# Four closing transposes of a triangular inverse as pieces of their own in an interleaved two-layer backbone kernel

## The chip, the core and the metric

The kernel runs on one core of one Trainium2 chip. The metric is the device time of one execution in microseconds (us). TensorE (PE) does the matmuls, VectorE (DVE), ScalarE (ACT) and GpSimd (POOL) the rest; SyncE (SP) and POOL issue most transfers. Each engine runs its own instructions in the order in which they stand in its stream.

## The reference

The reference is a flow-matching backbone of two layers over 512 latent tokens of width 1024, with a prefix of 256 context tokens. The even layer has two grouped-query attentions, the odd layer a 2-D neighbourhood attention beside a bidirectional recurrence (RWKV-7). Each layer ends in a SwiGLU. The part that matters here is the recurrence, run forward and backward over first the context and then the latent tokens, for 8 heads of 64:

```python
def wkv7_scan(state0, p, d, reverse, emit):
    ...
    def step(S, inp):
        w_t, k_t, v_t, kk_t, a_t = inp[:5]
        sa = jnp.einsum('bhvk,bhk->bhv', S, kk_t)
        S = (S * w_t[:, :, None, :] - sa[..., None] * (kk_t * a_t)[:, :, None, :]
             + v_t[..., None] * k_t[:, :, None, :])
        return S, (jnp.einsum('bhvk,bhk->bhv', S, inp[5]) if emit else None)

    s_fwd, yc_fwd = wkv7_scan(zero, cx, 0, False, need_ctx)
    s_bwd, yc_bwd = wkv7_scan(zero, cx, 1, True, need_ctx)
    _, y_fwd = wkv7_scan(s_fwd, lat, 0, False, True)
    _, y_bwd = wkv7_scan(s_bwd, lat, 1, True, True)
```

## The kernel before

**Dense work.** A projection takes its weights in tiles of 128 output columns. SP loads a tile (`wraw`), ACT casts it to a high part (`whi`, L143), DVE subtracts for the low part (`wlo`, L145), two buffers each. PE then forms three products: high by high (L422), activation low by weight high (L423), high by weight low (L424). L119 and L124 split an activation in the same way.

**The recurrence in chunks of 32 tokens.** For the context (256 tokens) and for each of two groups of latent tokens, `prepare` builds decay products (L1231 to L1250 on ACT and DVE), the scaled keys `kb` (L1242), the Gram blocks `G` (matmul L1258, mask L1262) and their transposes (L1260). Then `rwkv_inverse` inverts 32 unit triangular blocks of 32x32 per head half and direction: two POOL memsets (L1291, L1292), four DVE transposes from `G` (L1295), 31 rank-1 steps of a product and a subtraction (L1299, L1302), and four transposes of the result back into `G` (L1307). It is a generator that pauses after every second rank-1 step, 15 times. The caller then spills `G` to HBM (L1515, SP), from where `rwkv_load` (L1323) fetches each chunk's operands for the scan.

**The scan.** One step handles one chunk for both directions: W from VU and Sd (matmuls L1351, L1357, copies L1361, L1365), VU from W (L1370, L1373), the new state S (L1380, L1381), its scaled copies Sd (L1384) and, for latent tokens, the outputs (L1389, L1391).

**What sets the order.** The work is written as Python generators, and one runs beside another by counts: a main loop calls `step(n)` after each of its pieces, and the aside generator is advanced by the whole part of what it is owed. In layer 0's FFN the aside is the context chain (its projections, its inverse, its scan), advanced by 1.6 pieces for each FFN piece (L968), with a modulation row beside it for every second piece (L956). `finish` flushes what is left behind layer 1's first norm. In layer 1, latent group 0 advances the dense projections by 0.1 for each inverse piece (L1636). Group 1 is interleaved with the first half of the latent scan: after each scan piece it is owed 1.75 pieces, and each of them advances the dense projections by 1.4 (L1645 to L1652). A list scheduler then reorders the instructions of a block by its own costs. `keep_in_program_order` adds an edge without a semaphore: its instruction may not stand ahead of the instruction written before it on the same engine. The modulation rows (L278) have it already.

**After group 1** the neighbourhood attention starts beside the second half of the scan: scores (L1087), their bias and row maximum (L1092 on DVE), exponentials (L1093), transposes (L1099), copies of these (L1101 on DVE) and the products with the values (L678).

Of the kernel before, what the change touches and what calls it, by code (L numbers as in the profile page):

```python
# [69 lines left out]
class Net:  # L70
# [1203 lines left out]
    def rwkv_inverse(self, kbp, tp, Gs):  # L1274


        nc, V = self.nc, self.nc.vector
        L = self.t(kbp, [P, 1024], "kb").rearrange("p (a b) -> p a b", a=32)
        Xf = self.t(kbp, [P, 1024], "kb")
        X = Xf.rearrange("p (a b) -> p a b", a=32)  # L1280
        M = self.t(tp, [P, 256], "pi", bufs=1)

        def blocks(t, d, u):
            q = 32 * (2 * d + u)
            return t[q : q + 32, ::-1, ::-1] if d else t[q : q + 32]

        def inG(d, u):
            W = Gs[d].shape[3]
            return Gs[d][HD * u + 32 : HD * u + HD].rearrange("p c a t -> p t c a")[:, W - 32 : W]

        nc.gpsimd.memset(Xf, 0.0)  # L1291
        nc.gpsimd.memset(Xf[:, 0:1024:33], 1.0)  # L1292
        for d in range(2):
            for u in range(2):
                V.transpose(blocks(L, d, u), inG(d, u))  # L1295
        for j in range(31):
            n, m = 31 - j, j + 1
            t = M[:, 0 : n * m].rearrange("p (a b) -> p a b", a=n)
            V.tensor_tensor(  # L1299
                t, L[:, j + 1 : 32, j : j + 1].broadcast_to([P, n, m]), X[:, j : j + 1, 0:m].broadcast_to([P, n, m]), op=ALU.mult  # L1300
            )
            V.tensor_tensor(X[:, j + 1 : 32, 0:m], X[:, j + 1 : 32, 0:m], t, op=ALU.subtract)  # L1302
            if j % 2:
                yield
        for d in range(2):
            for u in range(2):
                V.transpose(inG(d, u), blocks(X, d, u))  # L1307

    def rwkv_state(self, sp):

# [517 lines left out]
```

## Time and profile before

| what | value |
|---|---|
| median of three runs | 2051.96 us (2051.79 to 2053.8) |
| profiled execution | 2053.72 us, of which span 2051.9 |
| PE busy | 1956.0 us (95%) |
| DVE busy | 1261.4 us (61%) |
| ACT, POOL busy | 893.7 us, 163.0 us |
| closing transposes (L1307) | 12, of 1877 to 2083 ns each |
| where they stand | 987 to 999 us (context), 1354.8 to 1362.8 (group 0), 1484.0 to 1491.7 (group 1) |

Times in rows of the timeline count from the start of the span, the second number is the duration in us. In brackets stand the idle time of that engine just before, and what ended it. A row with `x4` is a run of four instructions. The windows view gives busy times per engine for a stretch, then PE's granted clock as a share of full speed, then the busy share of the DMA engines and GB/s.

### The profile page before, as it was taken

To read this page: it belongs to the slowest core of one execution; us is meant where nothing else is said; L and a number is where in the kernel's file an instruction comes from. 1 tells how busy PE (TensorE), PEld (TensorE's weight loads), DVE (VectorE), ACT (ScalarE), POOL (GpSimd) and SP (SyncE) were. 2 spreads that over 40 slices of the span, in tenths; PEclk is the share of its full clock that TensorE was granted. 3 is DMA by queue.
4 is the path that set the end of the run, shared out by engine and by line. 5 is a ranking of instruction groups with operands and counts; after the bars stand their busy time and mean duration, and the time that the engine had idled before them with its cause. 6 is when DMAs were issued, how large, how long until landed. Compare 5 with 4: busy or idle time off the path is not lost.

```text
span 2051.9 us, 37913 instructions
## 1 busy us (share of the span) xinstructions
PE 1956.0 (95%) x15360; PEld 1606.6 (78%) x15360; DVE 1261.4 (61%) x2504; ACT 893.7 (44%) x1681; POOL 163.0 (8%) x326
## 2 busy tenths in 40 slices
PE   7999999999988999999999999899899989999997
PEld 6776778999987888777777777677667778888887
DVE  5656667666657554659746767787757773333335
ACT  4335556766733433553222346545345453222221
POOL 0111100000010001000112000102322000000000
PEclk9999999999999999999999999999799999999999
DMA  7453422434484345545533323455665133332321
GB/s 277 148 182 124 145 91 74 145 115 128 133 268 141 109 128 164 157 147 154 179 125 117 111 73 98 130 173 174 171 198 146 52 98 113 93 101 85 106 90 50
DMA packets 109918, 272.64 MB, mean 133 GB/s; under 512 B 14736, under 2 KB 48176, under 8 KB 106800
## 3 DMA queue, kind: packets, MB, share of 16 engines
q1 hardware_dynamic: 97520, 224.74, 35.5%
q0 software_dynamic: 12224, 45.49, 6.8%
q8 instruction: 121, 1.98, 0.4%
q14 instruction: 53, 0.43, 0.1%
HBM read 238.20 MB, written 31.98 MB: 132 GB/s over the span
## 4 chain that ended last, share of the span: by engine, by line
PE 78%; DVE 10%; issue 6%; DMA 3%; ACT 2%; POOL 0%; DVEq 0%; ACTq 0%; SPq 0%; POOLq 0%
PE ps_b L422 17%; PE ps_b L423 17%; PE ps_b L424 17%; PE ps_v L678 4%; PE ps_a L628 2%; PE ps_e L650 2%; PE ps_w L1351 2%; PE ps_w L1357 2%; DVE wlo L145 1%; PE ps_s L1380 1%; DMA xx<-in_wmod 1%; PE ps_w L1370 1%; PE ps_e L1258 1%; PE ps_w L1389 1%; DVE kb L1295 1%
## 5 line engine op out<-in xcount | busy, mean ns | idle before, releaser
L143 ACT CAST whi<-wraw 128x1024 fp32r<-128x1024 f32 (+2 forms) x291 | 292.6, 1008 | 664.1 <-PE ps_b L423 526.3
L145 DVE TENSOR_TENSOR wlo<-wraw,whi 128x1024 fp32r<-128x1024 f32 (+2 forms) x291 | 340.8, 1172 | 235.5 <-ACT whi L143 229.3
L422 PE MATMUL ps_b<-hxh,whi 128*128 128x512 f32 (+1 forms) x1040 | 402.4, 390 | 15.8 <-ACT cj L1018 6.7
L423 PE MATMUL ps_b<-hxl,whi 128*128 128x512 f32 (+1 forms) x1040 | 398.4, 385 | 2.1 <-DVE hxl L415 1.9
L424 PE MATMUL ps_b<-hxh,wlo 128*128 128x512 f32 (+1 forms) x1040 | 396.6, 383 | 2.2 <-DVE wlo L145 2.2
L422 PEld LDWEIGHTS ps_b<-hxh,whi 128*128 128x128 f32 x1040 | 199.1, 193 | 59.0 <-ACT cj L1018 7.2
L423 PEld LDWEIGHTS ps_b<-hxl,whi 128*128 128x128 f32 x1040 | 199.2, 192 | 40.7 <-DVE hxl L415 3.8
L424 PEld LDWEIGHTS ps_b<-hxh,wlo 128*128 128x128 f32 x1040 | 199.5, 193 | 39.7 <-DVE wlo L145 3.3
L422 PE MATMUL ps_b<-act,whi 128*128 128x512 f32 (+1 forms) x570 | 198.9, 349 | 6.5 <-ACT whi L143 3.3
L424 PE MATMUL ps_b<-act,wlo 128*128 128x512 f32 (+1 forms) x570 | 197.4, 346 | 2.1 <-DVE wlo L145 2.1
L423 PE MATMUL ps_b<-act,whi 128*128 128x512 f32 (+1 forms) x570 | 196.4, 345 | 0.4 <-DVE act L124 0.4
L422 PE MATMUL ps_b<-hch,whi 128*128 128x256 f32 x552 | 159.9, 290 | 4.2 <-ACT cj L982 2.1
L424 PE MATMUL ps_b<-hch,wlo 128*128 128x256 f32 x552 | 156.4, 284 | 0.8 <-DVE wlo L145 0.7
L423 PE MATMUL ps_b<-hcl,whi 128*128 128x256 f32 x552 | 156.0, 283 | 0.0
L422 PEld LDWEIGHTS ps_b<-act,whi 128*128 128x128 f32 x570 | 109.2, 192 | 21.7 <-issue 4.3
L424 PEld LDWEIGHTS ps_b<-act,wlo 128*128 128x128 f32 x570 | 109.1, 191 | 16.1 <-DVE wlo L145 3.3
L423 PEld LDWEIGHTS ps_b<-act,whi 128*128 128x128 f32 x570 | 109.1, 191 | 13.3 <-DVE act L124 0.8
L754 DVE TENSOR_TENSOR ff_a<-ff_a,ps_b 128x512 f32<-128x512 f32 x44 | 30.2, 687 | 134.3 <-PE ps_b L424 133.6
L422 PEld LDWEIGHTS ps_b<-hch,whi 128*128 128x128 f32 x552 | 104.9, 190 | 8.7 <-ACT cj L982 2.6
L424 PEld LDWEIGHTS ps_b<-hch,wlo 128*128 128x128 f32 x552 | 104.7, 190 | 1.9 <-DVE wlo L145 1.5
L455 DVE SCALAR_TENSOR_TENSOR xx<-ps_b,mod,xx 128x512 f32<-128x512 f32 (+1 forms) x64 | 43.7, 684 | 101.0 <-PE ps_b L424 100.6
L423 PEld LDWEIGHTS ps_b<-hcl,whi 128*128 128x128 f32 x552 | 105.1, 191 | 0.9 <-issue 0.2
(375 smaller groups left out, 3332.2 us busy)
## 6 DMA issues: line engine op xcount, KB each, us to landing
wraw<-in_ffi SPq DMA_DIRECT2D x132, 512.0 KB, 3.6
xx<-in_wmod POOLq DMA_DIRECT2D x48, 512.0 KB, 4.9
wraw<-in_w1in SPq DMA_DIRECT2D x43, 512.0 KB, 3.7
wraw<-in_ffo SPq DMA_DIRECT2D x48, 448.0 KB, 3.3
wmod<-in_wmodT POOLq DMA_DIRECT2D x32, 512.0 KB, 3.9
wraw<-in_ffo SPq DMA_DIRECT2D x24, 512.0 KB, 3.6
op<-op SPq DMA_DIRECT2D x32, 384.0 KB, 3.8
qx<-in_wmod SPq DMA_DIRECT2D x8, 1024.0 KB, 10.6
```

The costliest lines, as they stand in the source:

```text
L143: self.nc.scalar.copy(hi[:, 0:n], raw)
L145: e.tensor_tensor(lo[:, 0:n], raw, hi[:, 0:n].bitcast(F32), op=ALU.subtract)
L422: mm(out, lhsT=wh, rhs=hh, start=first, stop=False)
L423: mm(out, lhsT=wh, rhs=hl, start=False, stop=False)
L424: mm(out, lhsT=wl, rhs=hh, start=False, stop=last)
L455: self.nc.vector.scalar_tensor_tensor(X[:, m, c], ps[:, 0:n][:, c], gate[:, m, i : i + 1], X[:, m, c], op0=ALU.mult, op1=ALU.add)
L628: nc.tensor.matmul(o, lhsT=q, rhs=k[:, b : b + o.shape[1]], start=i == 0, stop=i == len(passes) - 1)
L650: nc.tensor.transpose(pt[:, P * (j - c) : P * (j - c) + P], p[:, P * j : P * j + P], self.ident)
L678: self.nc.tensor.matmul(ps[HD * u : HD * u + HD, col : col + P], lhsT=vs[u][j], rhs=pts[u][:, j, :], start=j == 0, stop=j == nk - 1, tile_ ...
L754: V.tensor_tensor(a, a, pg[1][:, 0:w], op=ALU.mult)
L1351: mm(wy[HD * u + HD - W_ + r : HD * u + HD, p, :], lhsT=G[top[u], p, r:W_], rhs=VU[top[u], p, u, :], start=p == 0, stop=False, skip_group_ ...
L1357: mm(o, lhsT=AR[:, p, :], rhs=Sd[:, p, u, :], start=False, stop=not lat, skip_group_check=True)
```

## The change

Each of the four closing transposes is tied behind the DVE instruction written just before it, and the generator pauses after each. The inverse so has 19 pauses instead of 15, in all three of its uses.

```diff
@@ -1304,7 +1304,8 @@
                 yield
         for d in range(2):
             for u in range(2):
-                V.transpose(inG(d, u), blocks(X, d, u))
+                self.tc.keep_in_program_order(V.transpose(inG(d, u), blocks(X, d, u)))
+                yield
 
     def rwkv_state(self, sp):
```

Lines from 1308 on are one higher in the changed kernel. The order of the instructions changes at three places and around them.

On DVE in the context's inverse, inside layer 0's FFN (`xx` is the residual stream, `wmod` a modulation row), the rows before:

```order
L1302 TENSOR_TENSOR kb_10271<-kb_10271,pi_10272 128x31
L1307 STREAM_TRANSPOSE G_1908_9355<-kb_10271 32x32x32
L455 SCALAR_TENSOR_TENSOR xx_7182<-ps_b_10565,mod_8_79,xx_7182 128x512
L145 TENSOR_TENSOR wlo_10638<-wraw_10635,whi_10637 128x896
L1307 STREAM_TRANSPOSE G_1908_9355<-kb_10271 32x32x32
L1307 STREAM_TRANSPOSE G_1909_9356<-kb_10271 32x32x32
L455 SCALAR_TENSOR_TENSOR xx_7182<-ps_b_10601,mod_8_79,xx_7182 128x512
L145 TENSOR_TENSOR wlo_10671<-wraw_10668,whi_10670 128x896
L1307 STREAM_TRANSPOSE G_1909_9356<-kb_10271 32x32x32
```

and of the change, from the second of its transposes on:

```order
L455 SCALAR_TENSOR_TENSOR xx_7182<-ps_b_10713,mod_8_79,xx_7182 128x512
L1307 STREAM_TRANSPOSE G_1908_9355<-kb_10271 32x32x32
L279 ISA wmod_10593,mod_9_80<-wmod_10593,silu_r_8030,c_tab_65 128x1024
L279 ISA mod_9_80 128x1
L1307 STREAM_TRANSPOSE G_1909_9356<-kb_10271 32x32x32
L145 TENSOR_TENSOR wlo_10775<-wraw_10772,whi_10774 128x1024
```

The first transpose keeps its place; the other three have moved behind the next weight tiles, and other work stands between each two of them. The context chain is four pieces longer with it: on PE, the L1351 and L1357 of its last step stood ahead of the last tiles of layer 0's FFN, and the last step but one and this one now stand behind them, among the matmuls of layer 1's first norm.

On ACT in latent group 0, two sets of decay operations and the evacuation of a dense tile (`cj` from PE's bank `ps_b`), before:

```order
L1240 ACTIVATE P_1522_7226<-sg_13859 128x8x32
L1231 ACTIVATE th_13911<-ps_e_13907,b0h_7220 128x256
L1231 ACTIVATE th_13911<-ps_e_13908,b0h_7220 128x256
L1233 ACTIVATE sg_13914<-th_13911,half_7218 128x256
L1235 ACTIVATE KA_13916<-th_13911,omka_7223,kah_7222 128x8x32
L1236 ACTIVATE KA_13916<-th_13911,half_7218 128x8x32
L1240 ACTIVATE P_1522_7226<-sg_13914 128x8x32
L1018 ACTIVATE cj_13937<-ps_b_13770 128x8x64
L143 CAST whi_14126<-wraw_14124 128x1024
```

and of the change:

```order
L1240 ACTIVATE P_1522_7226<-sg_13865 128x8x32
L143 CAST whi_14126<-wraw_14124 128x1024
L1018 ACTIVATE cj_13914<-ps_b_13770 128x8x64
L1231 ACTIVATE th_13934<-ps_e_13930,b0h_7220 128x256
L119 CAST cj_13913<-cj_13914 128x512
```

The cast and the evacuation have moved from behind the second set to ahead of it. On DVE, one `wlo` and one L124 now stand among the last rank-1 steps of that inverse, and its four transposes stand together as before.

On DVE at the end of latent group 1, where the attention's scores begin, before:

```order
L1092 ISA hxl_2795_15655,sm_m_15654<-ps_a_15651,cb_15588,big_15579 128x512
L1092 ISA sm_m_15654 128x1
L1302 TENSOR_TENSOR kb_14897<-kb_14897,pi_14898 128x31
L1092 ISA hxl_2800_15689,sm_m_15688<-ps_a_15685,cb_15588,big_15579 128x512
L1092 ISA sm_m_15688 128x1
L1307 STREAM_TRANSPOSE G_2577_13847<-kb_14897 32x32x32 x2
L1307 STREAM_TRANSPOSE G_2578_13848<-kb_14897 32x32x32 x2
L1101 COPY hxh_2801_15692<-ps_e_15693 128x512
```

and of the change:

```order
L1302 TENSOR_TENSOR kb_14910<-kb_14910,pi_14911 128x3x29
L1101 COPY hxh_2801_15692<-ps_e_15693 128x512
L1299 TENSOR_TENSOR pi_14911<-kb_14909,kb_14910 128x60
L1092 ISA hxl_2815_15783,sm_m_15782<-ps_a_15779,cb_15588,big_15579 128x512
L1092 ISA sm_m_15782 128x1
L1302 TENSOR_TENSOR kb_14910<-kb_14910,pi_14911 128x2x30
L1299 TENSOR_TENSOR pi_14911<-kb_14909,kb_14910 128x31
L1302 TENSOR_TENSOR kb_14910<-kb_14910,pi_14911 128x31
L1307 STREAM_TRANSPOSE G_2577_13853<-kb_14910 32x32x32 x2
L1307 STREAM_TRANSPOSE G_2578_13854<-kb_14910 32x32x32 x2
L1101 COPY hxh_2811_15772<-ps_e_15773 128x512
```

Before, two score operations stood ahead of the transposes and the first L1101 behind them. Now five score operations and the first L1101 stand among the rank-1 steps ahead of them, and the second L1101 behind.

## The prediction

> **What bounds the kernel now.** I read the page's engine totals first, then the windows around the three inverses, then the timeline inside those windows.
>
> ```profile
> PE 1956.0 (95%) x15360; PEld 1606.6 (78%) x15360; DVE 1261.4 (61%) x2504; ACT 893.7 (44%) x1681; POOL 163.0 (8%) x326
> L1307 DVE STREAM_TRANSPOSE G<-kb x12: 1877/1986/2083, 987.1 to 1489.8; 32x1024 f32<-32x1024 f32 x12
> ```
>
> TensorE is busy 95% of the span. A change that adds no matmul can gain only where PE stands idle, some 96 us in all, and can lose wherever it makes PE stand. The twelve closing transposes cost DVE 12 x 1.99 = 24 us; the change removes none of that. It moves them, and what stands around them.
>
> ```profile
> 1140.00:1160.00 20.00, 20.00 (x229) 15.69 (x228) 12.51 (x22) 5.95 (x11) 1.83 (x3) 1.00 0.25 80
> 1168.00:1192.00 24.00, 19.37 (x164) 16.51 (x158) 21.48 (x61) 11.37 (x24) 1.52 (x2) 0.93 0.36 132
> 1380.00:1400.00 20.00, 20.00 (x356) 15.25 (x357) 14.33 (x31) 10.09 (x25) 8.18 (x12) 1.00 0.63 179
> 1422.00:1441.00 19.00, 16.80 (x119) 13.00 (x116) 17.45 (x32) 3.96 (x7) 2.98 (x6) 0.82 0.68 200
> 1501.00:1620.00 119.00, 118.21 (x1707) 86.39 (x1704) 80.50 (x177) 61.80 (x145) 28.64 (x48) 1.00 0.43 121
> ```
>
> After each stretch stand its length, then busy us of PE, weight loads, DVE, ACT and POOL, then the granted clock. In the FFN of layer 0 (1140), between the two latent groups (1380) and in the attention (1501) PE is full at clock 1.00. What is gained ahead of such a stretch carries to the end. In layer 1's first norm (1168) DVE is the busy one: 21.48 of 24 us, with PE 4.63 us idle. Those idle places are what the change can touch.
>
> **Part A: the context inverse, the FFN and the norm.** The four pauses added here lengthen the aside generator by four pieces, and half-rate modulation rows run with it. The FFN advances the aside at its own rate, so its last pieces no longer fit. One whole step of the context scan and the first half of the next now stand behind the FFN, in the norm.
>
> ```profile
> 1154.69 0.64 PE L1351 MATMUL ps_w<-VU,op 32*32 32x64 f32 x16
> ...
> 1156.40 0.64 PE L1357 MATMUL ps_w<-Sd,op 128*32 128x64 f32 x16
> 1167.66 1.08 PE L1370 MATMUL ps_w<-W,op 32*32 32x64 f32 x32
> 1152.26 0.69 PE L1380 MATMUL ps_s<-VU,op 128*64 128x64 f32 x16
> 1192.09 0.50 PE L422 MATMUL ps_b<-hxh,whi 128*128 128x512 f32 x1 [1.88 <-ACT wa L1147]
> 1190.78 1.22 DVE L145 TENSOR_TENSOR wlo<-wraw,whi 128x1024 fp32r<-128x1024 f32 x1 [1.67 <-ACT whi L143]
> 1171.11 0.43 DVE L1373 COPY VU<-ps_w 32x256 f32<-32x256 f32 x1
> ```
>
> The first half of a step (four sets, from 1154.69 to 1157.04) takes 2.3 us of PE; L1370 takes 1.1, the two sets of L1380 2 x 0.69. So 4.8 us for a step and 2.3 for the half: 7.1 us leave a stretch where PE is full. The norm has 4.63 us of PE idle, so at least 2.5 of the 7.1 come back. DVE has as many S and Sd operations between its first and last hxl as before, since the new step takes the slot of the old one. But the second step's end now falls at the start of the dense phase: two W copies (2 x 0.43) ahead of the wlo of 1190.78, mostly in its 1.67 us idle, and two VU copies behind it. They end near 1190.78 + 1.22 + 0.86 = 1192.9. PE's L1380 waits for them ahead of the first dense matmul, which stood at 1192.09. With its own 0.7 that puts the dense start at 1193.6, 1.5 us late. I take A = 7.1 - 2.5 - 1.5 = **+3.1 us**. Bounds: +4.6 if the late copies hide, and -4 if none of the 7.1 hides (0) and a load is waited for (3.8, below). The spread transposes are worth at most the stall behind them:
>
> ```profile
> 996.07 0.47 PE L422 MATMUL ps_b<-act,whi 128*128 128x512 f32 x1 [0.47 <-DVE xx L455]
> ```
>
> That is 0.47 us once; I count nothing, because the copies now between the transposes meet other late tiles.
>
> **Part B: latent group 0.** The four transposes stay back to back on DVE; the four new pauses only pull the dense stream forward.
>
> ```profile
> 1322.24 0.42 ACT L1240 ACTIVATE P<-sg 128x256 f32<-128x256 f32 x1 [3.19 <-DVE sg L1237]
> 1326.64 1.08 ACT L1018 ACTIVATE cj<-ps_b 128x512 f32<-128x512 f32 x1
> 1327.78 0.80 PE L422 MATMUL ps_b<-hxh,whi 128*128 128x512 f32 x1 [5.26 <-ACT cj L1018]
> 1336.59 1.23 DVE L145 TENSOR_TENSOR wlo<-wraw,whi 128x1024 fp32r<-128x1024 f32 x1 [2.24 <-ACT whi L143]
> 1354.80 7.99 DVE L1307 STREAM_TRANSPOSE G<-kb 32x1024 f32<-32x1024 f32 x4
> 1362.82 0.69 DVE L1242 TENSOR_TENSOR kb<-KA,pi 128x512 f32<-128x512 f32 x1
> 1363.56 1.97 PE L1258 MATMUL ps_e<-AR,kb 64*64 64x64 f32 x32 [3.45 <-DVE kb L1242]
> 964.83 0.39 PE L424 MATMUL ps_b<-act,wlo 128*128 128x512 f32 x1
> ...
> 968.23 0.39 PE L424 MATMUL ps_b<-act,wlo 128*128 128x512 f32 x1
> ```
>
> ACT's L1018, which frees PE's bank, moves ahead of the second set of decay operations and no longer waits for that set's L1237. It can start once the first set's L1240 (done at 1322.66) and one weight cast are through, up to 3 us earlier; I take 1.8, since nothing here shows that cast's own operands that early. PE restarts near 1326.0, and the whi that DVE awaits for 2.24 us comes 1.8 earlier too. DVE spends that on the one wlo (1.22) and the one L124 (0.68) now ahead of the transposes, 1.9 us in all. So the transposes and L1258 keep their times, and PE enters L1258 with 14 matmuls of the next tile done instead of 2. A matmul of the dense rows takes (968.23 - 964.83) / 15 = 0.227 us, so 12 are 2.7 us out of the idle time. I take **+2.0**, as L1258 and its followers run slow after a pause. Bounds: +3.1 with L1258 also 0.4 earlier; -1.2 if the 1.9 us on DVE is not covered and ACT's second set, now behind L143 and L1018, is 2 us late.
>
> **Part C: latent group 1.**
>
> ```profile
> 1422.87 1.98 DVE L1295 STREAM_TRANSPOSE kb<-G 32x1024 f32<-32x1024 f32 x1
> 1424.90 5.94 DVE L1295 STREAM_TRANSPOSE kb<-G 32x1024 f32<-32x1024 f32 x3
> 1428.74 1.22 PE L1389 MATMUL ps_w<-VU,op 32*32 32x64 f32 x22
> 1432.13 0.41 DVE L1381 TENSOR_TENSOR S<-ps_s,S 128x256 f32<-128x256 f32 x1
> 1432.15 0.80 PE L424 MATMUL ps_b<-hxh,wlo 128*128 128x512 f32 x1 [2.20 <-DVE wlo L145]
> 1484.01 7.69 DVE L1307 STREAM_TRANSPOSE G<-kb 32x1024 f32<-32x1024 f32 x4
> 1486.47 0.43 PE L678 MATMUL ps_v<-hxh,cv 128*64 128x128 f32 x2
> 1492.47 1.12 PE L678 MATMUL ps_v<-hxh,cv 128*64 128x128 f32 x8 [5.57 <-DVE hxh L1101]
> 1494.54 1.05 PE L1099 MATMUL ps_e<-ident,hxl 128*128 128x128 f32 x4
> 1493.52 1.22 PE L1087 MATMUL ps_a<-ck,cq 128*128 128x512 f32 x2
> ```
>
> The dense stream is still ahead, by about 15 matmuls, when the opening transposes start. The wlo that stood behind them stands before them now, so its 2.20 us stall goes. Next late is the S update behind the transposes: from the first L1295's start DVE needs 8.0 (1422.87 to 1430.84), 0.68 (L124, an operation as large as L1242) and 0.41, or 9.1 us, with a short rank-1 product between. PE has 20 matmuls (4.5) and a set of L1380 and L1389 (0.69 + 1.22) to do, 6.4. That is a stall of some 3 us: 2.20 - 3.0 = **-0.8**. At the end five score copies (L1092) and one L1101 stand ahead of the closing transposes instead of two and none. While DVE transposes, PE has 8 of L678, 8 of L1099 and 3 of L1087 to do: 1.1 + 2.1 + 1.8 = 5.0 us, against 1484.01 to 1486.90 = 2.9 before. So the 5.57 us wait shrinks by 2.1. C = **+1.3**. Bounds: +4.3 (no new stall, 2.2 + 2.1), and -3 (the new stall in full, the closing group 2.2 us late behind the three extra copies).
>
> Sum: 3.1 + 2.0 + 1.3 = 6.4 us off the profiled execution's 2053.72 us (span 2051.9). The median of the three runs is 2051.96; the same 6.4 off it gives **2045.6**.
>
> One rule of the Trainium skill bears on C. Its page "TensorE: Matmul & The Clock Gate" (section "What's actually happening") says PE drops to half clock after an idle window of about 3.4 us. The matmul at 1432.15 took 0.80 us after only 2.20 us of waiting, so this trace does not follow it to the letter. By the rule a 3 us stall costs no clock, and the sum would be that of the third rival.
>
> **The rivals.**
>
> First, *the gains cancel*. In two of three inverses the transposes do not spread, which is against the change doing what it says; what is pulled forward is then owed later, since PE's work is the same. If B and C yield nothing and A only its bare 0.47, it is 2051.5. Against it: PE is full from 1380 to 1420, so what is done earlier is not waited for there.
>
> Second, *the context steps hold the norm* (slower). PE takes its matmuls in order. The two steps' operand loads now come among the loads of layer 1's weights:
>
> ```profile
> wraw<-in_w1in SPq DMA_DIRECT2D x43, 512.0 KB, 3.7
> op<-op SPq DMA_DIRECT2D x32, 384.0 KB, 3.8
> ```
>
> If a load is one place late, PE stands 3.8 us in front of the norm's matmuls with the 7.1 us of steps unhidden, and the dense start is 1.5 us later: +5.3 us, 2057.3 with B and C at zero. It decides from about 3 us of late load on. For it: PE waits at L1370 and L1380 already cost 0.71 and 1.16 us in this stretch:
>
> ```profile
> 1169.45 0.33 PE L1380 MATMUL ps_s<-VU,op 128*64 128x64 f32 x2 [0.71 <-ACT VU L1373]
> 1170.94 0.34 PE L1380 MATMUL ps_s<-VU,op 128*64 128x64 f32 x4 [1.16 <-DVE VU L1373]
> ```
>
> Against it: these loads wait for no result of the norm.
>
> Third, *the clock stays up*. The stretch 1422 to 1441 ran at 0.82, which costs 19 x 0.18 = 3.4 us. If PE never pauses long there, 2045.6 - 3.4 = 2042.2; with the stall gone too it is near 2039.
>
> **How the numbers follow.** The forecast gets 0.45 (own range 2042 to 2049), the first rival 0.20, the second 0.17, the third 0.18. About 0.2% (4.1 us) is what a measurement of this kernel can tell from none, so faster means below 2047.9. Faster: 0.85 of 0.45 and the 0.18 = 0.56. Slower (above 2056.1): most of the second rival, and mixtures of it with lost ground in C, 0.16. Same: the rest, 0.28. The range runs from 2039 (third rival) to 2054 (the second rival with part of B and C).
>
> **What would show it.** A: the FFN ends about 7 us earlier, and the first 128x512 matmul behind the norm comes 3 us earlier than 1192.1. B: the wait in front of PE near 1327 falls to about 3.5 us, L1258 stays near 1363 less A, and its wait grows to some 7 us. C: no wait on wlo behind L1295, a wait on L1380 instead, and the wait on L1101 near 3.5 us. Wrong would be a wait for a DMA at L1351 in the norm, or closing transposes of group 1 that start no earlier than 1484.

## The result and the profile after

| kernel | median, us | executions | ratio to before, 95% interval |
|---|---|---|---|
| before, beside it | 2053.2 (2050.77 to 2061.81) | 8 | |
| changed | 2070.56 (2059.61 to 2075.85) | 8 | 1.0068 [1.0052, 1.0084] |

The change makes the kernel slower by 0.68%, some 14 us (the interval spans 11 to 17 us). Forecast were 6.4 us less. The executions of the changed kernel spread widely: the three shortest had a mean granted clock of 0.969 to 0.971, the four longest 0.960 to 0.965. The profiled one is a short one (2062.75 us, span 2061.0), so ratios carry the verdicts below, and single profiles show only places.

The page and the form-by-form groups of the changed kernel:

```profile
span 2061.0 us, 37920 instructions
PE 1959.5 (95%) x15360; PEld 1611.0 (78%) x15360; DVE 1261.0 (61%) x2504; ACT 893.4 (43%) x1681; POOL 162.0 (8%) x326
L1307 DVE STREAM_TRANSPOSE G<-kb 32x1024 f32<-32x1024 f32 x12 | 23.8, 1987 | 0.3
```

Work and transposes are what they were (PE 1956.0 and DVE 1261.4 us busy before; 1.99 us for each transpose). Of the 9.1 us that the span grew, PE is busy in 3.5 and idle in 5.6. So it is order, in two regions.

**The context, the FFN and the norm.** Timeline of the changed kernel: the first, third and last transpose, the spill of `G` and the loads of the scan's first operands (SP's queue), then PE's waits, then the last dense matmul of the FFN and the first of 128x512 behind the norm:

```profile
988.66 2.08 DVE L1307 STREAM_TRANSPOSE G<-kb 32x1024 f32<-32x1024 f32 x1
...
1010.96 2.04 DVE L1307 STREAM_TRANSPOSE G<-kb 32x1024 f32<-32x1024 f32 x1
...
1022.37 2.08 DVE L1307 STREAM_TRANSPOSE G<-kb 32x1024 f32<-32x1024 f32 x1
...
1024.48 0.54 SPq L1516 DMA_DIRECT2D op<-G  x1
1028.48 1.97 SPq L1324 DMA_DIRECT2D op<-op  x4
...
1014.31 0.50 PE L424 MATMUL ps_b<-hxh,wlo 128*128 128x512 f32 x1 [1.71 <-DVE wlo L145]
1032.99 0.81 PE L1352 MATMUL ps_w<-VU,op 32*32 32x64 f32 x16 [2.48 <-DVE wlo L145]
...
1165.18 0.28 PE L424 MATMUL ps_b<-act,wlo 128*128 128x256 f32 x1
...
1195.61 0.50 PE L422 MATMUL ps_b<-hxh,whi 128*128 128x512 f32 x1
```

The stretch of the two waits in both windows views, the changed kernel and then the kernel before (columns as in the prediction: PE's busy time comes first behind the length, the granted clock third from the end), and before's last dense matmul of the FFN:

```profile
1000.00:1040.00 40.00, 35.81 (x198) 28.85 (x197) 22.45 (x24) 9.23 (x12) 1.58 (x3) 0.92 0.53 171
```

```profile
1000.00:1040.00 40.00, 39.83 (x345) 31.34 (x344) 20.93 (x30) 10.80 (x17) 5.35 (x8) 1.00 0.55 172
```

```profile
1167.45 0.28 PE L424 MATMUL ps_b<-act,wlo 128*128 128x256 f32 x1
```

Spread over 34 us of a stretch in which PE was full (39.83 of 40 us before), the transposes bring PE two waits, and the clock falls to 0.92. The first, 1.71 us, is for a `wlo`: two transposes and a modulation row stand on DVE ahead of it, and it starts at 1013.03. The second, 2.48 us, the view puts down to a `wlo` as well, but in a second profile of the same kernel (e4 below) the scan's first matmuls stand so:

```profile
1030.01 0.64 PE L1352 MATMUL ps_w<-VU,op 32*32 32x64 f32 x16 [1.95 <-issue]
```

The `wlo` of that place ends behind it there (1028.95 + 1.23 us), so it can't be what PE waited for. It was the load of the scan's first operands: the last transpose ends at 1024.45, the spill is issued at 1024.48, the loads from 1028.48 on, and by the trace's semaphores the first of them lands at 1032.59, 0.40 us ahead of L1352. In e4 that distance is 0.40 us too, in e1 0.49.

From the FFN's last dense matmul to the first of 128x512 behind the norm it takes 24.6 us before (to 1192.09, a row of the prediction) and 30.4 after. The FFN ends 2.3 us earlier, and the dense work of layer 1 starts 3.5 us late instead of 3.1 early.

**The latent groups.** Timeline of the changed kernel, PE and DVE:

```profile
1328.58 0.79 PE L422 MATMUL ps_b<-hxh,whi 128*128 128x512 f32 x1 [3.60 <-ACT cj L1018]
1367.63 1.84 PE L1258 MATMUL ps_e<-AR,kb 64*64 64x64 f32 x32 [3.79 <-DVE kb L1242]
...
1432.15 1.98 DVE L1295 STREAM_TRANSPOSE kb<-G 32x1024 f32<-32x1024 f32 x1
1441.36 0.69 PE L1381 MATMUL ps_s<-VU,op 128*64 128x64 f32 x16 [2.10 <-DVE S L1382]
...
1491.59 0.74 DVE L1092 CUSTOM_DVE_ANT_1 hxl<-ps_a,cb,big 128x512 f32<-128x512 f32 x1
...
1493.72 0.75 DVE L1092 CUSTOM_DVE_ANT_1 hxl<-ps_a,cb,big 128x512 f32<-128x512 f32 x1 [0.33 <-PE ps_a L1087]
1495.53 0.75 DVE L1092 CUSTOM_DVE_ANT_1 hxl<-ps_a,cb,big 128x512 f32<-128x512 f32 x1 [0.89 <-PE ps_a L1087]
1496.37 0.69 DVE L1101 COPY hxh<-ps_e 128x512 f32<-128x512 f32 x1
1498.62 7.74 DVE L1307 STREAM_TRANSPOSE G<-kb 32x1024 f32<-32x1024 f32 x4
1507.13 1.97 PE L678 MATMUL ps_v<-hxh,cv 128*64 128x128 f32 x14 [5.31 <-DVE hxh L1101]
```

And the kernel before, its first score reduction:

```profile
1482.27 0.75 DVE L1092 CUSTOM_DVE_ANT_1 hxl<-ps_a,cb,big 128x512 f32<-128x512 f32 x1 [0.33 <-issue]
```

From group 1's opening to the first score reduction it takes 1482.27 - 1422.87 = 59.4 us before and 1491.59 - 1432.15 = 59.4 after. Of the dense matmuls 46 stand in this stretch before and 31 after: 15 (15 x 0.227 = 3.4 us by the prediction's row) left it and stand ahead of it. The stretch did not get shorter, its start got later. From the first score to the closings it takes 1.7 us before and 7.0 after. The opening is 9.3 us late, the closings 14.6, and the end 9.1. A wait of PE for a load of the attention ahead of its first scores, 3.44 us in this profile, is in neither e4 nor e11 below, and the stretch takes 60.6 us in both: that load is not the price.

### The profile page after: what moved, and what is told of

Same layout as the page of the kernel before. It is cut to its first block, busy times and chain, and to the rows that moved or that the text cites. A ratio compares the mean times of both kernels' runs of the same rounds, so it can differ in the third digit from the quotient of the medians.

```text
span 2061.0 us, 37920 instructions
## 1 busy us (share of the span) xinstructions
PE 1959.5 (95%) x15360; PEld 1611.0 (78%) x15360; DVE 1261.0 (61%) x2504; ACT 893.4 (43%) x1681; POOL 162.0 (8%) x326
## 4 chain that ended last, share of the span: by engine, by line
PE 78%; DVE 9%; issue 6%; DMA 3%; ACT 2%; POOL 0%; SPq 0%; DVEq 0%; ACTq 0%; POOLq 0%
PE ps_b L422 18%; PE ps_b L423 17%; PE ps_b L424 17%; PE ps_v L678 4%; PE ps_a L628 2%; PE ps_e L650 2%; DVE wlo L145 2%; PE ps_w L1352 1%; PE ps_s L1381 1%; PE ps_w L1358 1%; PE ps_e L1258 1%; DMA xx<-in_wmod 1%; PE ps_a L1087 1%; PE ps_w L1371 1%; ACT whi L143 1%
```

## Experiments

One point needs no run: with the change made in group 1 only, every engine has the instruction order of the kernel before, and so it has with the ties in all three uses and no pauses. So the tie acts only together with the pause, and group 1 gets its new order, the seam before the attention included, from the pauses of group 0: in its trace e2 below, with the change in group 0 alone, has the order of the changed kernel from latent group 0 on. The runs take the parts apart from there. All ratios are to runs of the kernel before on the same chip.

**Context alone, with and without the tie.** `inverses` counts the three uses (0 context, 1 and 2 the latent groups):

```diff
+        k = self.inverses = getattr(self, "inverses", -1) + 1
-                V.transpose(inG(d, u), blocks(X, d, u))
+                x = V.transpose(inG(d, u), blocks(X, d, u))
+                if k in (0,):        # e1; in e3: never
+                    self.tc.keep_in_program_order(x)
+                if k in (0,):
+                    yield
```

> The change in the context's inverse alone (its four closing transposes tied and paused after; the two latent inverses as before). Theory: the loss has two separate parts, and this one is that the spread transposes stand ahead of a weight subtraction that PE waits for: two stalls of 1.7 and 2.5 us near 1014 and 1033 with a slow clock behind the second, while 7 us of scan work hide in the norm only in part. In the changed kernel group 0 starts 2.8 us later than before, so 2.5 to 4 us slower here, 2055 us. Rival (the loss is all in the latent groups, and the context part only shifts where it shows): within 1 us of before.

Measured: 2058.16 us, ratio 1.0019 [1.001, 1.0028].

> The pauses in the context's inverse, without the ties: the scan steps move from the FFN to the norm as in the change, but the four transposes are free to stand where the scheduler puts them, the last two together. Theory (the spread transposes cost, the move of the steps gains): the stalls of 1.7 and 2.5 us go, 0 to 3 us faster than before, about 2050.5. Rival (the move of the steps costs by itself): as the context alone, 2.5 to 4 us slower.

Measured: 2052.72 us, ratio 0.9995 [0.9983, 1.0007]. PE's waits in the FFN, with the tie and then without it, and at the end of the latter the FFN's last dense matmul and the first of 128x512 behind the norm:

```profile
1012.58 0.50 PE L424 MATMUL ps_b<-hxh,wlo 128*128 128x512 f32 x1 [1.71 <-DVE wlo L145]
1031.48 0.81 PE L1356 MATMUL ps_w<-VU,op 32*32 32x64 f32 x16 [2.74 <-DVE wlo L145]
```

```profile
1005.19 0.47 PE L422 MATMUL ps_b<-act,whi 128*128 128x512 f32 x1 [1.60 <-DVE xx L455]
...
1161.58 0.28 PE L424 MATMUL ps_b<-act,wlo 128*128 128x256 f32 x1
...
1193.97 0.50 PE L422 MATMUL ps_b<-hxh,whi 128*128 128x512 f32 x1
```

The pauses move the scan steps behind the FFN in both. Without the tie the norm then takes 32.4 us instead of 24.6, so what leaves the FFN comes back there, and no gain is clear of noise (the interval reaches from 3.5 us faster to 1.4 slower). The tie makes the two waits, on a `wlo` and on the scan's first operands, and costs the difference, 0.24%, some 5 us.

**Group 0 alone, and the whole change again.** As above with `k in (1,)`; the second is the changed kernel itself.

> The change in the inverse of latent group 0 alone; context and group 1 as before. By the order of the instructions the change in group 1 alone moves nothing, so this part holds all that the latent groups lose. Theory: the 0.4 more pieces of dense work that are drawn forward delay the opening transposes of group 1, and the stretch from there to the attention isn't bound by PE (late operand loads of the attention, the inverse on DVE), so the work drawn forward isn't got back: 5 to 8 us slower, about 2058. Rival (work drawn forward is got back, as the prediction had it): 1 to 3 us faster, about 2050.

Measured: 2071.52 us, ratio 1.0078 [1.0052, 1.0104]. Slower, as the theory had it, but by at least twice what it expected.

> The whole change once more. Its times so far fall in two groups, near 2060 and near 2075 us, with no die to tell them apart on one core. Theory: the two parts add (3 and 6 us) to about 2061, and the upper group is a second course of the attention's start behind group 1, where the profile has a wait of 3.4 us for a load: a profile of the upper group would show its 14 us there, between 1440 and 1540. Rival: the upper group loses everywhere a little, by a lower granted clock.

Measured: 2072.83 us, ratio 1.0072 [1.0044, 1.0099]. This profile is of a long execution, with a span of 2071.9 us against 2061.0 and the same order on DVE, ACT and POOL. Its opening stands 5.6 us later than in the first profile, its closings 6.8, and the rest is 4.1 longer. So the theory of one late load between 1440 and 1540 missed. The two losses lie where the granted clock is low with PE nearly full: 0.57 from 1400 to 1420 (last section) and 0.83 from 1520 to 1540.

Group 0 alone costs as much as the whole, within the intervals. DVE in e2's profile:

```profile
1431.40 1.98 DVE L1295 STREAM_TRANSPOSE kb<-G 32x1024 f32<-32x1024 f32 x1
...
1495.99 0.69 DVE L1101 COPY hxh<-ps_e 128x512 f32<-128x512 f32 x1
...
1498.21 7.71 DVE L1308 STREAM_TRANSPOSE G<-kb 32x1024 f32<-32x1024 f32 x4
```

The opening is 8.5 us late and the closings 14.2, with nothing changed in the context: the span is 2066.2, 14.3 over before. Not all of the 8.5 is the change's. The clock from 1400 to 1420 is 0.83 here and was 1.00 before; e12 below, whose DVE and ACT have before's order up to there, opens at 1426.05, 3.2 us late, with a clock of 0.85. Some 5 us are left for the work drawn forward.

**Less dense work ahead.** If work drawn forward costs, work held back might gain. After group 0 the dense stream is owed one piece less, or four:

```diff
+            self.owed += -1.0        # e5; in e6: -4.0
```

> The kernel before, with the dense projections of layer 1 owed one piece less once latent group 0 is written (the change there is the same as 0.4 pieces more: the instruction order of both comes out identical). So the dose goes the other way: six dense matmuls of the last tile now stand behind the first scan step past the opening transposes. Theory (granted clock: the scan's matmuls of 32 and 64 rows don't hold the clock up, dense ones between them do, and what is drawn forward is missing there): the full-speed us lost to the clock between 1420 and 1560, 17 in the profile before, fall, and the time is 0 to 4 us below before. Rival (any move of the order from the tuned one costs, through the waits at the seam with the attention): slower by 2 us or more.

Measured: 2054.48 us, ratio 1.0005 [0.9992, 1.0018].

> As the run before it, but owed four pieces less: sixteen dense matmuls are spread over the first four scan steps behind the opening transposes. Granted-clock theory: less clock lost than with one piece, 2 to 6 us below before. Rival (waits at the seam): slower, and more so than with one piece.

Measured: 2054.26 us, ratio 0.9998 [0.9986, 1.0009]. Neither the gain nor the loss that the two theories expected came. Both kernels also have four reductions of L1092 ahead of the closings and no copy, so four reductions there cost nothing that can be measured.

**Filling group 1 with matmuls.** Once the dense stream has run out, small matmuls stand alone in this stretch, and the granted clock falls there. In the changed kernel, by its windows:

```profile
1480.00:1500.00 20.00, 17.48 (x136) 12.29 (x136) 12.36 (x34) 7.21 (x18) 4.72 (x10) 0.56 0.22 71
```

That is 0.56 with PE busy 17.48 of 20 us, a rival cause of the loss. These kernels leave nothing out; they add matmuls into a bank that nobody reads, three for each scan piece (30 in all, 30 x 0.227 = 6.8 us), to group 0's change (e7) and to the kernel before (e8):

```diff
+                if not self.later:
+                    ps = self.bank("b")
+                    for q in range(3):
+                        self.tc.keep_in_program_order(
+                            nc.tensor.matmul(ps, lhsT=hx[0][0][:, 0:P], rhs=hx[0][1 + q], start=q == 0, stop=q == 2)
+                        )
```

> The change in group 0 alone, and after each scan piece of group 1's stretch in which the dense stream is used up three extra 128x512 matmuls into an unread PSUM bank, some thirty in all, 6.8 us of PE at full clock. They add work that nothing needs, and they also push the first L1101 behind the closing transposes. Granted-clock theory: the time stays at or below that of the change in group 0 alone (2071 median), its spread of 20 us shrinks, and the clock lost between 1420 and 1560 falls from 27 by 10 or more. Rival (PE's waits and work make the time, the clock only follows): 5 to 8 us slower than the change in group 0 alone.

Measured: 2059.9 us, ratio 1.0026 [1.001, 1.0043].

> The kernel before with the same extra matmuls; here all score copies come to stand behind the closing transposes. Granted-clock theory: the 17 us of clock lost between 1420 and 1560 fall by about the 6.8 us that are added, so within 4 us of before. Rival (the clock doesn't matter): 5 to 8 us slower than before.

Measured: 2054.77 us, ratio 0.9997 [0.9987, 1.0008]. DVE in the two, e7 and then e8:

```profile
1426.17 1.99 DVE L1296 STREAM_TRANSPOSE kb<-G 32x1024 f32<-32x1024 f32 x1
...
1487.66 7.69 DVE L1309 STREAM_TRANSPOSE G<-kb 32x1024 f32<-32x1024 f32 x4
1495.38 0.69 DVE L1102 COPY hxh<-ps_e 128x512 f32<-128x512 f32 x1
```

```profile
1420.88 1.98 DVE L1296 STREAM_TRANSPOSE kb<-G 32x1024 f32<-32x1024 f32 x1
...
1480.49 7.77 DVE L1308 STREAM_TRANSPOSE G<-kb 32x1024 f32<-32x1024 f32 x4
```

In e8, 6.8 us of added matmuls cost nothing: opening to closings takes 59.6 us against 61.1 (the two reductions, 1.7 us, stand behind the closings there). Dense work does not set this stretch, so taking some out of it, as the change does, could gain nothing either. In e7 five of the seven or eight tenths of a per cent are back. It looks like the clock, but the filler had also moved the scheduler's order: the first copy of L1101 now stands behind the closings, and three reductions ahead of them instead of five. Two more runs hold that order as group 0's change has it, with 20 matmuls (`range(2)`) and with 30 of 32 columns (`ps[:, 0:32]`, `rhs[:, 0:32]`).

> The change in group 0 alone with two extra 128x512 matmuls after each of those scan pieces, twenty in all, 4.5 us of PE at full clock. With two instead of three, DVE keeps the order of the change in group 0 alone at the seam: five score copies and the first L1101 ahead of the closing transposes. So this tells the clock from the seam. Granted-clock theory: 3 to 9 us faster than the change in group 0 alone (median 2071), though work was added, and the upper group of its times gets rarer. Rival (what helped with three matmuls was the order at the seam): 2071 plus up to 4.5 us.

Measured: 2070.37 us, ratio 1.0072 [1.0046, 1.0099].

> The change in group 0 alone with thirty extra matmuls at the same places, of 32 columns instead of 512: as many instructions, next to no work for the array, and the order at the seam of the change in group 0 alone. Granted-clock theory: within 2 us of the change in group 0 alone, its spread unchanged. Rival (any instruction between the scan's matmuls keeps PE awake, or shifts the order in a helpful way): as fast as with the matmuls of 512 columns.

Measured: 2071.81 us, ratio 1.008 [1.0059, 1.0101]. DVE in e9, where the copy is ahead of the closings again:

```profile
1429.30 1.99 DVE L1296 STREAM_TRANSPOSE kb<-G 32x1024 f32<-32x1024 f32 x1
...
1491.86 0.69 DVE L1102 COPY hxh<-ps_e 128x512 f32<-128x512 f32 x1
...
1493.71 7.71 DVE L1309 STREAM_TRANSPOSE G<-kb 32x1024 f32<-32x1024 f32 x4
```

Filler without the other order gains nothing. It did raise the clock where it stands, to 0.81 from 1480 to 1500 in e9 against 0.59 in e2. So the low clock of this stretch is not by itself the price, and the order at the seam is left. That the clock matters behind the closings is not ruled out by this, and the last rows of the next part bear on it.

**The copy on another engine.** ScalarE takes the attention's first two blocks of transposed probabilities, so no copy stands ahead of the closings on DVE. The reductions stay. First on group 0's change, with its control on the kernel before:

```diff
-                ev = V.tensor_copy if u else nc.scalar.copy
+                k = self.evs = getattr(self, "evs", -1) + 1
+                ev = V.tensor_copy if u and k > 1 else nc.scalar.copy
```

> Group 0 alone has the pauses and ties, and in addition ScalarE, instead of VectorE, evacuates the first two blocks of transposed probabilities of the attention, so that no copy of L1101 stands ahead of the closing transposes of group 1 on VectorE (the five reductions of L1092 still do). Theory that the closings are late because this copy waits there for TensorE: from the opening of group 1 to its closings 59 to 63 us, the closings start before 1491, and the time is 2056 to 2063, about that of the version with 30 extra matmuls (2059.9). Rival that the five reductions are enough to make them late: 64 to 68 us, 2066 to 2072. Rival that the dense work drawn forward ahead of group 1 costs by itself: the 60 to 63 us may come, but the time stays at 2066 to 2072, because the rest after the closings grows.

Measured: 2062.69 us, ratio 1.0036 [1.002, 1.0052].

> The kernel before with the same change of engine for the first two evacuations alone, as the control of the run beside it. In the kernel before the first copy of L1101 already stands behind the closing transposes, so every theory expects the time of before within 0.3% (2047 to 2060) and 59 to 63 us from opening to closings; if the change of engine alone is worth more than that, the run beside it has to be compared with this one and not with before.

Measured: 2052.1 us, ratio 0.9992 [0.998, 1.0003]. DVE in e11, and its span:

```profile
1433.44 1.98 DVE L1296 STREAM_TRANSPOSE kb<-G 32x1024 f32<-32x1024 f32 x1
...
1494.01 0.74 DVE L1092 CUSTOM_DVE_ANT_1 hxl<-ps_a,cb,big 128x512 f32<-128x512 f32 x1
...
1501.28 7.74 DVE L1309 STREAM_TRANSPOSE G<-kb 32x1024 f32<-32x1024 f32 x4
1509.06 0.69 DVE L1102 COPY hxh<-ps_e 128x512 f32<-128x512 f32 x1
```

```profile
core 0: 2063.5 us, clock 0.965
```

The time came as the theory said, the mechanism did not: opening to closings still takes 67.8 us, and the first reduction still stands 7.3 us ahead of the closings. So the reductions make the closings late, and the copy costs elsewhere. Since this run's interval only touches that of group 0 alone, the same edit was made on the whole change and on e9's kernel:

> The whole change, and ScalarE evacuates the attention's first two blocks of transposed probabilities, so that no copy of L1101 stands ahead of the closing transposes of group 1. Theory that this copy, standing there, carries about half of the loss: 2058 to 2065 (1.003 to 1.005, of which 0.002 for the ties in the context). Rival that what it stands for in the run with group 0 alone was chance, and the five reductions and the dense work drawn forward carry the loss: 2068 to 2074, as without it. In both the closings start 64 to 68 us after the opening, since the reductions stand where they stood.

Measured: 2061.52 us, ratio 1.0052 [1.0033, 1.007].

> The pauses and ties in group 0 alone, 20 extra matmuls into an unread bank in group 1, and ScalarE evacuates the attention's first two blocks. Without that last edit the time was 2070.37, with five reductions and one copy ahead of the closings; now four reductions and no copy stand there. If the copy and the fifth reduction carry half of the loss: 2056 to 2064. If the dense work drawn forward carries it: 2068 to 2073.

Measured: 2061.65 us, ratio 1.0032 [1.0021, 1.0044]. The traces of e9 and e14 both have five reductions ahead of the closings, not four as this expectation says of e14. Closings and span of e13, then of e14:

```profile
1494.70 7.71 DVE L1308 STREAM_TRANSPOSE G<-kb 32x1024 f32<-32x1024 f32 x4
```

```profile
core 0: 2056.0 us, clock 0.973
```

```profile
1498.68 7.71 DVE L1310 STREAM_TRANSPOSE G<-kb 32x1024 f32<-32x1024 f32 x4
```

```profile
core 0: 2060.3 us, clock 0.972
```

Without a copy ahead, the ratio falls each time: 1.0078 to 1.0036, 1.0068 and 1.0072 to 1.0052, 1.0072 to 1.0032. The last pair's intervals are apart; in the others they overlap. From the start of the closings to the end of the span the three profiles without it take 2063.5 - 1501.28 = 562.2, 561.3 and 561.6 us. With it, group 0 alone takes 568.0 (2066.2 - 1498.21) and e9, whose span is 2068.0, 574.3, but the changed kernel's own profile, a short execution, 562.4. The kernel before, which has no copy ahead either but less of the attention done by then, takes 2051.9 - 1484.01 = 567.9. So the copy's place goes with some 0.2% to 0.4% of the time, and not by making the closings late. DVE and ACT also change their order at 19 and 13 places up to 1620 us with this edit, and the copy is not separated from these.

The profiles show where the difference lies. PE is full behind the closings in both e9 and e14, here e9 and then e14, but the granted clock is not the same, and 370 matmuls stand in the one window and 549 in the other:

```profile
1520.00:1550.00 30.00, 30.00 (x370) 22.68 (x364) 11.60 (x28) 10.81 (x28) 8.61 (x15) 0.54 0.54 137
```

```profile
1520.00:1550.00 30.00, 30.00 (x549) 23.32 (x546) 17.54 (x39) 14.63 (x39) 11.78 (x20) 0.94 0.65 162
```

Counted at full speed, what the clock takes from 1520 to 1560 is 0 in the changed kernel's first profile, 3.4 us in its second and in e10, 6.8 in e2 and 13.8 in e9, and the stretch from the closings to the end takes 562.4, 566.5, 565.7, 568.0 and 574.3. In the three without the copy ahead it is 0, 0 and 1.8. Over all executions the median of the mean clock is 0.962 to 0.969 in the five series with the copy ahead (the changed kernel twice, e2, e9, e10), 0.969 to 0.972 in the three without, and 0.973 to 0.974 in the kernel before. So the copy's part of the loss goes with a lower clock behind the closings; why the clock falls there more often with the copy ahead is open.

## Why the prediction was wrong

**A, the context: forecast +3.1, measured a loss.** Two steps failed. The one that makes the loss is "The spread transposes are worth at most the stall behind them", 0.47 us, of which it counts nothing. Each is a 2 us block on DVE where PE was full (39.83 of 40 us). Two of them made a `wlo` late by 1.71 us. The last one made the spill late, and with it the load of the scan's first operands, for which PE stood 2.48 us. With the ties the context part costs 0.19% (3.9 us), without them nothing that is clear of noise.

The other is the term "at least 2.5 of the 7.1 come back". The forecast let 4.0 us come back (2.5, and 1.5 at the dense start); the norm took 5.8 us longer in the changed kernel and 7.8 without ties. So nearly all that left the FFN came back, though times alone can't exclude the 3.1 us (0.9995, down to 0.9983).

The lower bound of -4 us had the size, and both its conditions came near: the steps stay unhidden, and a load is waited for. But that load is the first one behind the last transpose, in the FFN; in the norm PE's longest wait is 0.94 us, for a copy of W. The second rival has the right sign and kind of wait for this part in the wrong place.

**B, group 0: the mechanism right, its worth wrong.** The wait near 1327 fell from 5.26 to 3.60 us (forecast 3.5), because L1018 moved. The wait at L1258 rose from 3.45 to 3.79, not to 7; why PE's lead came out smaller stays open. L1258 itself came 4.1 us later than before; the dense work of layer 1 had already started 3.5 us late. The failed step is "12 are 2.7 us out of the idle time", carried to the end. Work drawn forward is a gain only if the place it leaves is bound by it. That place, from group 1's opening to the first scores, takes 59.4 us with it or without it, and e8 put 6.8 us of matmuls in for nothing. I had argued that PE is full from 1380 to 1420; it is, but past 1422 dense matmuls are not the bound. That the 62 dependent operations of the inverse on DVE and the scan steps between them are it fits the order, and is argued, not shown.

**C, group 1: the waits right, the sum wrong.** The 2.20 us on `wlo` went, a new wait on S took its place (2.10, forecast some 3). The wait on L1101 is 5.31, not 3.5, and the closings start at 1498.62, which the prediction had named as a sign of error (no earlier than 1484). The mis-sized term is "the closing group 2.2 us late behind the three extra copies". What the runs show in its place has two sides: from the first score to the closings it takes 7.0 us instead of 1.7, for three more reductions, the copy, and waits for the scores in PE (0.33 and 0.89 us); and the copy ahead was counted as a gain of 2.1 but goes with a loss of 0.2% to 0.4%. The prediction counts this order under group 1; it comes from the pauses of group 0.

**The sum.** Context 1.0019 and group 0 1.0078 are not apart from the whole, 1.0068 and 1.0072, by their intervals. Of group 0's part, about half goes with the copy's place. What is left, 1.0026, 1.0036 and 1.0032 in the three versions without it, is some 6 us. The later opening (3.4 us of dense matmuls ahead of it, and a lower clock) and the reductions ahead of the closings are both in it. Since e7 has three reductions ahead and e11 five at nearly the same ratio, and e5 and e6 have four at no cost, the opening is the likelier of the two; that is argued, not shown.

The third rival, the clock stays up, went the other way: the median of the mean clock is 0.962 in e4's series of the changed kernel and 0.973 in the kernel before beside it. The first rival's point, that B and C only shift work, held, but it took the seam to be free.

## What to carry to other kernels

Before counting work drawn forward as a gain, ask what bounds the stretch it leaves: dense matmuls in a stretch that they do not set are free there, as 6.8 us of them were here, and 3.4 us of them moved ahead of it made its start later and the stretch no shorter. A tie that spreads a block of in-order DVE work is paid where that engine hands tiles to a full PE, and again behind the last piece, where a spill and a load wait for the whole block. A wait that a view puts down to one engine is worth a second look in another execution: here it was that load. When one count in an interleaving changes, look for the new order at the seams downstream, even one group away, and cost the work that now stands ahead of the operation on which the next stage waits.

## What the hardware showed

The granted clock fell with PE busy all the time. Two windows between the latent groups, in the second profile of the whole change and in the first:

```profile
1400.00:1420.00 20.00, 20.00 (x180) 13.78 (x174) 9.45 (x22) 7.43 (x18) 2.05 (x4) 0.57 0.29 77
```

```profile
1400.00:1420.00 20.00, 20.00 (x291) 14.73 (x288) 13.70 (x32) 11.78 (x27) 4.25 (x8) 0.98 0.52 133
```

In the same program, PE is busy 20.00 of 20 us in both, and the clock is 0.57 in one and 0.98 in the other; 180 matmuls stand in the one window and 291 in the other. The Trainium skill's page "TensorE: Matmul & The Clock Gate" (section "What's actually happening") puts the lower clock after an idle window of about 3.4 us, which would ask for an idle stretch just ahead. By the same windows view the twenty microseconds ahead (1380 to 1400) are full at clock 1.00 in both profiles:

```profile
1380.00:1400.00 20.00, 20.00 (x388) 15.41 (x389) 13.59 (x29) 12.78 (x32) 6.35 (x11) 1.00 0.51 131
```

So this trace does not agree with that rule as far as busy time in the profile tells, and the measurement decides. The same page of the Trainium skill also says that the window runs freely, so that where it begins differs from run to run; that would fit the spread between executions (2059.61 to 2075.85 us at clocks from 0.971 to 0.960), but no run here shows the window.
